# First two MLP pairs with eight plain products, residual added by accumulating transfers, residual stream kept in the output (hybrid decoder layer, 1024 tokens)

## Chip, cores and metric

One core of one Trainium2 chip runs the kernel. The metric is device time of one execution in microseconds (us); lower is better. Engines: PE is TensorE, DVE VectorE, ACT ScalarE, POOL GpSimd, SP SyncE, which here only issues transfers.

## The reference

One decoder layer over T = 1024 tokens of D = 1024 features, in float32. A mixer (S5 state space group and short convolution group) ends in an output projection, a norm and a residual add; a gated MLP with a convolution of width 3 over time follows:

```python
y = concatenate([head_rms_norm(y_a, ...), head_rms_norm(y_b, ...)], axis=-1)
x = x + gt1 * rms_norm(y @ w_out[i], g_post_mix[i])
h = rms_norm(x, g_pre_ffn[i]) * (1.0 + sc2) + sh2
hid = causal_dwconv(h @ w_up, ffn_conv_w)      # w_up: 1024 x 5632
a, v = split(hid, 2)
x = x + gt2 * rms_norm((silu(a) * v) @ w_down, g_post_ffn[i])   # w_down: 2816 x 1024
```

## The kernel before

**Arithmetic.** A float32 product is made of three fast products, high x high, high x low, low x high (`mm3`, L472; lines 476, 478, 480). So every operand is split: a cast gives the high half (weights: ACT, L462 or L1888), a subtraction the low half (DVE or POOL). A split weight tile of 128 x 1024 lies in a buffer `hl` (three of them), its raw form in a buffer `w` ("raw", three of them).

**Layout and order.** Features lie on partitions, tokens along the columns. The whole program is written by generators (`t_...`), each with a priority; a scheduler (`Flow`, L202) steps them by an internal list of costs and so writes one static order of instructions for each engine. An instruction that waits holds up all that stand behind it on its engine. Generators wait for events (`fire`) and for slots of buffers (`get`, `put`); `yield ("land",)` waits until a transfer has landed, and `SITES` (L89) says which engines a tensor operation may go to.

**Output projection and residual.** It goes by three token blocks (`blocks`): block 0 is the first token half (512 columns), blocks 1 and 2 are the quarters of the second half. `t_out` does the products of a block (weights `w_out` streamed for each block), squares and sums give the norm, and `t_x2` (L1700) makes the new residual `og` for two features groups at once (1024 or 512 columns): scale `og`, add x, square into the tile `xr` (ACT, L1710), store `og` to the scratch `x2_dr`, and sum the squares. x has been loaded before by SP into the tables `CL`, `Tr`, `Tz`, `St`, which are `xr` (`t_xr`, L1682). The sum over features is a matmul with a ones column (L492), its broadcast another (L502). `t_h2` (L1651) then gives the MLP's input, split into `h2h` and `h2l`.

**MLP, up.** 22 pairs: pair i has a tile a (128 columns of `w_up`) and a tile b (128 columns, the gated part), each with two halves of K, and the input has two token halves: a 2 x 2 block product. With Winograd's form of Strassen's scheme it takes seven products of 12 matmuls with 512 columns, not eight. The input blocks used are A11 and A12 (first token half, K halves), A22, and the sums S1 to S4 (`t_forms`); block A21 is only part of sums. The weights need sums too (`t_pair_weights`, L1901): differences on `w`, from them `wf` (split of the sum T2, for the product with S2), `hm` (split of the sum t, for S1 and A22) and the split of tile b. `t_combine` (L2011) adds the products up. For pairs 0 and 1, `t_ahead` (L1758) puts the products of A11 and A12 with tile a before the rest, since they need only the first token half; pair 0's remaining products are done in two halves of 256 columns, one for each block. `t_conv2` and `t_gate2` do the convolution (`cv`), silu and product; `t_sums` writes the results to the scratch `g_dr`.

**Residual, transposed.** The output has tokens on partitions. `t_x2t` (L2091) therefore loads pieces of `x2_dr`, transposes them on PE (16 groups of four transposes, spread over the first MLP pairs), copies each on ACT (`xt`), and stores it to the scratch `x2t_dr`.

**MLP, down.** `t_down` (L2220) does seven products in a row, P4 last, for four token groups `tb` each; w_down comes as `wd` (by SP and by POOL, L2195), split into `wh` and `wl` (DVE, L868). In the last product each token group keeps its last `LATE` = 3 steps of K for the end, so that the groups end one after the other. For each of the eight output rows of tiles `t_final` (L2329) loads the residual, waits for the halves, and does residual + u * r on DVE (L871, one for each 512 columns), and SP stores it.

Of the kernel before, what the change touches and what calls it, by code (L numbers as in the profile page):

```python
# [11 lines left out]
F32 = mybir.dt.float32  # L12
# [6 lines left out]
P = 128  # L19
# [295 lines left out]
def hybrid_layer(ctx, tc, xT, w_adaT, w_ada0, w_u, w_bcv, w_out, w_up, w_down, glu_w, vec, ssm, con, out):  # L315
# [17 lines left out]
    fl = Flow({"k2": NK2, "k4": NK4, "hl": NHL, "raw": NRAW, "big": 3, "sm": 2, "nrm": 2, "s4": 0, "sn": 0, "wf0": 0, "wf1": 0, "hm0": 0, "hm1": 0, "cv": 0, "gs": 0, "t5": 0, **{t: 1 for t in tables}})  # L333
# [97 lines left out]
    x2t_dr = tc.dram_tile([NB, P, D], F32, name="x2t_dr")  # L431
# [1088 lines left out]
    forms = {name: [[None, None] for _ in range(NT)] for name in ("A11", "A12", "A22", "S1", "S2", "S3", "S4")}  # L1520
# [128 lines left out]
    def t_h2(bi, k, og, r2b, left):  # L1649
# [33 lines left out]
    def t_xr():  # L1683

        yield ("wait", ev_stat["a"])
        for bi, (hf, lo, hi) in enumerate(blocks):
            n = hi - lo
            for dp in range(NT):
                tag = ("CL", "Tr", "Tz", "St")[dp]
                yield ("get", tag)  # L1690
                xr = table(tag, [1024])[:, : 2 * n]
                yield L_(n)
                load(
                    xr.rearrange("p (a t) -> p a t", a=2),
                    xT[2 * dp * P : (2 * dp + 2) * P, hf * H + lo : hf * H + hi].rearrange("(a p) t -> p a t", a=2),
                )
                ev_xr[bi][dp].tile = xr, tag
                fl.fire(ev_xr[bi][dp], True)

    def t_x2(bi, dp, sl, n, og, r1, s2):  # L1700
# [7 lines left out]
        yield from T_("x2", og, og, xr, ADD, 2 * n)  # L1708
# [25 lines left out]
    NAHEAD = 2  # L1734
    for i in range(NAHEAD):
        want(("up", i), w_up[i])
# [10 lines left out]
    def product(o, w, form, last, s=None):  # L1747

        for k in range(NT):
# [5 lines left out]
            mm3([o], w[0][:, ks], w[1][:, ks], [f[0]], [f[1]], k == 0, k == NT - 1)  # L1755
            if last and s != 0:
                fl.put("s4" if form == "S4" else "k2", 2)

    def t_ahead():

        yield ("wait", ev_out)
        for i in range(NAHEAD):
            w = wev["up", i]
            yield ("wait", w[0])
            hl = w[1]
            yield ("get", "big", 2 - i)
            pair_a[i] = big()
            if i == 0:
                pair_b[i] = big()
            for j, o, c, form in ((1, (pair_a if i else pair_b)[i][:, H:], 0, "A11"), (2, pair_a[i][:, :H], 1, "A12")):  # L1770
                yield from product(o, [hl[:, x, c * H : (c + 1) * H] for x in range(2)], form, False)
                ev_p[i, j].tile = o
                fl.fire(ev_p[i, j])
            fl.put("hl")
# [29 lines left out]
    NCV, NGS, NSN = 5, 2, 2  # L1804
# [60 lines left out]
    def t_forms2(s, dp, a11, a12, a21, a22):  # L1865
# [3 lines left out]
        for d2 in range(2):  # L1869
            yield from form_parts("S3", 2 * dp + d2, s, a21[:, d2], None)  # L1870
        yield from dve_tt(a12, a12, a11, SUB, H)
        for d2 in range(2):
            yield from form_parts("S4", 2 * dp + d2, s, a12[:, d2], None)
        forms_left[0] -= 1
# [6 lines left out]
    def odd_even(what, i):  # L1881

        return ptile("ba"[i % 2 == 0], what, [2, 1024 if what == "hm" else H], F32R)
# [17 lines left out]
    def t_pair_weights(i):  # L1901
        ev = pw[i]
        yield ("wait", pw[i - 1]["loaded"] if i else wev["up", NAHEAD - 1][2])
# [8 lines left out]
        if i:  # L1912
            yield ("wait", pw[i - 1]["t"])
        if i >= NAHEAD:
            yield ("get", "hl")
            ev["a"].tile = hl_tile()
            yield from split(ev["a"].tile, wa, 1024, "split_a")
            fl.fire(ev["a"])
        b11, b21, b12, b22 = wa[:, :H], wa[:, H:], wb[:, :H], wb[:, H:]

        yield from TT_("wsum" if i else "split_d", b11, b12, b11, SUB, H)
        yield from TT_("wsum" if i else "split_d", b12, b22, b12, SUB, H)
# [4 lines left out]
        yield from TT_("wsum" if i else "split_d", b22, b22, b11, SUB, H)  # L1927
        yield ("get", f"wf{i % 2}")
        ev["T2"].tile = odd_even("wf", i)
        yield from split(ev["T2"].tile, b22, H)  # L1930
        fl.fire(ev["T2"])
        yield from TT_("wsum" if i else "split_d", b21, b21, b22, SUB, H)
        fl.put("raw")
        yield ("get", f"hm{i % 2}")
        ev["t"].tile = odd_even("hm", i)
# [4 lines left out]
    def subs(i):  # L1940

        return ((0, slice(0, 256)), (1, slice(256, H))) if i == 0 else ((None, slice(0, H)),)

    snap = {(i, x): Event() for i in range(NFF) for x in ("a", "b")}

    def t_up(i):
        ev = pw[i]
        last = i == NFF - 1

# [4 lines left out]
        outs = {}  # L1954

        def one(j, o, x, c, form, s, sl):
            yield ("wait", ev[x])
            yield from product(o[:, sl], part(x, c), form, last, s)
            if s != 0:
                ev_p[i, j].tile = o  # L1960
                fl.fire(ev_p[i, j])

        def single(j, x, c, form, s, sl):
            if not s:
                yield ("get", "sm")
                outs[j] = small()
            yield from one(j, outs[j], x, c, form, s, sl)

        if i < NAHEAD:
            yield ("wait", ev_p[i, 2])  # L1970
        else:
            yield from single(1, "a", 0, "A11", None, slice(0, H))
        for s, sl in subs(i):
            yield from single(6, "T2", 0, "S2", s, sl)
            if s != 0:
                fl.put(f"wf{i % 2}")
            yield from single(5, "t", 0, "S1", s, sl)
            if i >= NAHEAD:
                yield ("get", "big")
                pair_a[i] = big()  # L1980
                yield from one(2, pair_a[i][:, :H], "a", 1, "A12", None, slice(0, H))
                fl.put("hl")
            else:
                yield ("wait", ev_s1[i])
                yield from one(4, pair_a[i][:, H:], "t", 1, "A22", s, sl)
            if i not in pair_b:
                yield ("get", "big")
                pair_b[i] = big()
            yield from one(3, pair_b[i][:, :H], "b", 1, "S4", s, sl)
            yield from one(7, pair_b[i][:, H:], "b", 0, "S3", s, sl)  # L1990
            if s != 0:
                fl.put("hl")
            if i >= NAHEAD:
                yield from one(4, pair_a[i][:, H:], "t", 1, "A22", s, sl)
            if s != 0:
                fl.put(f"hm{i % 2}")

    def t_combine(i):
# [3 lines left out]
        su = ptile("a", "sn", [2, H], F32, NSN)  # L2002
# [3 lines left out]
        fl.fire(ev_s1[i])  # L2006
        if i >= NAHEAD:
            fl.put("sm")
# [20 lines left out]
    def cv(s):  # L2029
        return ptile("b", "cv", [T], F32, NCV)  # L2030

    def t_conv2(j, o):

        yield ("get", "cv")
        r = cv("cv")
# [7 lines left out]
    ev_gs = {(f, kk): Event() for f in FORM for kk in range(NKK)}  # L2043

    def t_gate2():
        even = None
        for i in range(NFF):
            yield ("wait", snap[i, "b"])
            b = yield from t_conv2(NFF + i, pair_b[i])
# [425 lines left out]
```

## Time and profile before

| what | value |
|---|---|
| time, median of 3 runs | 1159.94 us (1154.72 to 1162.32) |
| profiled execution: its time, and the span of the trace | 1158.81 us, 1157.0 us |
| busy share PE, DVE, ACT, POOL | 91%, 77%, 41%, 41% |
| mean granted TensorE clock, as a share of full speed | 0.954 |
| mean DMA rate | 152 GB/s |

The time of the profiled execution stands 1.8 us above its span. In time lines a row gives the start, the duration, the engine, the line, and output<-input; in brackets stands the idle time before it and what ended it. Matmul durations overlap, so their rate is read from their starts. "x4" is a row for four like instructions in a row, with their total.

### The profile page before, as it was taken

The numbers are of one execution on the slowest core, as the hardware profiler recorded it, in microseconds if no ns is written. First come the engines' busy times: TensorE is split into PE (matmuls) and PEld (weight loads), VectorE is DVE, ScalarE is ACT, GpSimd is POOL, SyncE is SP. The second block draws the span as 40 slices with busy tenths as digits, with TensorE's granted clock in tenths as the row PEclk, the third lists the DMA queues.
The fourth block names the chain that finished last, engine by engine and source line by source line (L and its number), as shares of the span: only waits on it lengthen the run. The fifth ranks groups of instructions, "written<-read, shape, count | busy, mean of one in ns | idle before, by whom it ended". The sixth has DMA issues, their size and how long they took to land. (4 is left out here: it accounts for less than half of the span.)

```text
span 1157.0 us, 13979 instructions
## 1 busy us (share of the span) xinstructions
PE 1049.7 (91%) x5000; PEld 849.2 (73%) x5000; DVE 893.4 (77%) x1237; ACT 476.1 (41%) x658; POOL 471.8 (41%) x464
## 2 busy tenths in 40 slices
PE   2888889899889988659999999999999999999995
PEld 2756678778546887557788888888888887888883
DVE  6769777887997389877787888888879977554855
ACT  4435422323244446444443434343434545454431
POOL 4799455671495034113534343434344320232000
PEclk9979889999898998769999999999999999999998
DMA  7633302237645256313463333233313698999344
GB/s 266 233 131 134 119 30 88 96 114 245 246 164 182 76 187 203 127 39 106 156 200 100 119 109 110 74 119 109 110 69 123 214 247 275 239 231 275 111 160 158
DMA packets 89973, 176.26 MB, mean 152 GB/s; under 512 B 8880, under 2 KB 34224, under 8 KB 89904
## 3 DMA queue, kind: packets, MB, share of 16 engines
q1 hardware_dynamic: 83568, 163.84, 41.0%
q0 software_dynamic: 6336, 11.54, 5.8%
q8 instruction: 39, 0.64, 0.2%
q14 instruction: 30, 0.25, 0.1%
HBM read 137.89 MB, written 37.46 MB: 152 GB/s over the span
## 5 line engine op out<-in xcount | busy, mean ns | idle before, releaser
L381 POOL TENSOR_TENSOR hl<-w,hl 128x1024 fp32r<-128x1024 f32 x38 | 98.4, 2590 | 245.0 <-ACT hl L1888 143.2
L381 POOL TENSOR_TENSOR w<-w,w 128x512 f32<-128x512 f32 x63 | 93.7, 1488 | 126.4 <-DVE hl L868 81.5
L871 DVE SCALAR_TENSOR_TENSOR cv<-big,vec,cv 128x896 f32<-128x896 f32 (+3 forms) x176 | 122.7, 741 | 4.1 <-ACT cv L2037 4.1
L1888 ACT CAST hl<-w 128x1024 fp32r<-128x1024 f32 (+1 forms) x67 | 68.6, 1024 | 53.9 <-issue 17.0
L2195 POOL DMA_DIRECT2D wd<-in_w_down_dram x44 | 38.6, 897 | 112.2 <-PE big L2244 29.4
L868 DVE TENSOR_TENSOR wl<-wd,wh 128x512 fp32r<-128x512 f32 x77 | 50.9, 687 | 36.3 <-ACT wh L2199 36.3
L476 PE MATMUL big<-s,hl 128*128 128x512 f32 (+1 forms) x184 | 71.2, 387 | 0.7 <-ACT xt L2110 0.7
L868 DVE TENSOR_TENSOR hl<-w,hl 128x1024 fp32r<-128x1024 f32 (+1 forms) x47 | 55.4, 1178 | 19.9 <-ACT hl L1888 19.9
L478 PE MATMUL big<-s,hl 128*128 128x512 f32 (+1 forms) x184 | 70.7, 384 | 0.0
L480 PE MATMUL big<-s,hl 128*128 128x512 f32 (+1 forms) x184 | 70.6, 384 | 0.0
L478 PE MATMUL big<-yl,hl 128*128 128x256 f32 (+1 forms) x192 | 63.8, 332 | 4.3 <-POOL yl L381 4.3
L2199 ACT CAST wh<-wd 128x512 fp32r<-128x512 f32 x77 | 46.4, 619 | 50.9 <-DMA wd<-in_w_down_dram 49.8
L476 PE MATMUL big<-yh,hl 128*128 128x256 f32 (+1 forms) x192 | 65.6, 342 | 1.3 <-ACT hl L462 1.1
L2037 ACT ACTIVATE cv<-big,vec 128x1024 f32<-128x1024 f32 x44 | 49.2, 1119 | 42.4 <-DVE big L868 33.6
L476 PE MATMUL big<-h,hl 128*128 128x512 f32 x192 | 63.0, 410 | 3.3 <-ACT h L724 1.5
L480 PE MATMUL big<-yh,hl 128*128 128x256 f32 (+1 forms) x192 | 63.8, 332 | 2.0 <-POOL hl L381 2.0
L480 PE MATMUL big<-h,hl 128*128 128x512 f32 x192 | 61.0, 400 | 2.8 <-POOL hl L381 2.8
L478 PE MATMUL big<-h,hl 128*128 128x512 f32 x192 | 60.9, 398 | 3.0 <-DVE h L726 3.0
L462 ACT CAST hl<-w 128x1024 fp32r<-128x1024 f32 x41 | 42.8, 1045 | 43.8 <-PE big L480 28.2
L868 DVE TENSOR_TENSOR hm<-w,hm 128x1024 fp32r<-128x1024 f32 (+1 forms) x39 | 45.9, 1177 | 11.3 <-ACT hm L1888 11.3
L2242 PE MATMUL big<-wh,hl 128*128 128x512 f32 x130 | 50.9, 391 | 1.3 <-DVE sn L868 0.8
L2244 PE MATMUL big<-wh,hl 128*128 128x512 f32 x130 | 50.8, 391 | 0.5 <-DVE hl L868 0.5
(351 smaller groups left out, 3114.2 us busy)
## 6 DMA issues: line engine op xcount, KB each, us to landing
w<-in_w_up_dram SPq DMA_DIRECT2D x46, 512.0 KB, 3.9
w<-g_dr SPq DMA_DIRECT2D x35, 512.0 KB, 5.6
g_dr<-cv SPq DMA_DIRECT2D x55, 256.0 KB, 2.3
wd<-in_w_down_dram SPq DMA_DIRECT2D x44, 256.0 KB, 6.8
wd<-in_w_down_dram POOLq DMA_DIRECT2D x44, 256.0 KB, 6.7
w<-in_w_out_dram SPq DMA_DIRECT2D x20, 512.0 KB, 3.5
WBT<-in_w_adaT_dram SPq DMA_DIRECT2D x16, 512.0 KB, 4.5
w<-in_w_bcv_dram SPq DMA_DIRECT2D x13, 512.0 KB, 3.4
```

The costliest lines, as they stand in the source:

```text
L381: {"dve": dve, "pool": pool}[e].tensor_tensor(o, a, b, op)
L462: act.copy(t[:, 0, :], w)
L476: pe.matmul(outs[i], wh, xh[i], start=start, stop=False)
L478: pe.matmul(outs[i], wh, xl[i], start=False, stop=False)
L480: pe.matmul(outs[i], wl, xh[i], start=False, stop=stop)
L868: (eng or dve).tensor_tensor(o, a, b, op)
L871: dve.scalar_tensor_tensor(o, a, s, b, op0, op1)
L1888: act.copy(t[:, 0, :n], w)
L2037: act.activation(r, o, AF.Copy, scale=V("ffn_conv_w", 3 * j + 2))
L2199: act.copy(hi, w)
L2242: pe.matmul(o, gh, wh, start=kk == 0, stop=False)
L2244: pe.matmul(o, gl, wh, start=False, stop=kk == NKK - 1)
```

## The change

1. *Eight plain products in pairs 0 and 1.* No weight sums, no combining: each pair's output is the plain sum of K halves in the same accumulator (A11 with A12, A22 with A21). The form A21 is now also made as a split. `t_ahead` does A11 and A12 for (pair 0, a), (0, b), (1, a); `t_first` the rest. Weight sums start with pair 2, whose order of products is 1624537 rather than 1652374, and whose sums run on DVE (site `split_d`).
2. *Residual added by transfers in blocks 0 and 1.* `t_xr` loads no x for them; `t_x2` issues from POOL a transfer of x that adds into `og`, and waits until it has landed. Block 2 is as before.
3. *Residual kept in the output.* `t_x2t` stores the transposed residual straight into the output. `t_final` scales on ACT and a POOL transfer adds the result into the output. The transposes take a small PSUM buffer. `LATE` is 7.
4. *Buffers.* Convolution tiles: 3 `cv` and 2 `ca` instead of 5 `cv`; `sn` moves to the later pool; S4 is formed before S3.

```diff
@@ t_h2
-        if hf and k < NT:
-            fl.fire(ev_h2[bi][k])
-            return
-        name = "A22" if hf else ("A11", "A12")[k // NT]
+        name = f"A{hf + 1}{k // NT + 1}"
@@ t_xr
-                yield L_(n)
-                load(
-                    xr.rearrange("p (a t) -> p a t", a=2),
...
+                if bi == 2:
+                    yield L_(n)
+                    load(xr.rearrange("p (a t) -> p a t", a=2), x_of(bi, dp))
@@ t_x2
-        yield from T_("x2", og, og, xr, ADD, 2 * n)
+        if bi == 2:
+            yield from T_("x2", og, og, xr, ADD, 2 * n)
+        else:
+            yield ("load", "pool", 1.0)
+            pool.dma_start(o3, x_of(bi, dp), accum_op=ADD)
+            yield ("land",)
@@ t_ahead
-        for i in range(NAHEAD):
...
+        for i, x, pair in ((0, "a", pair_a), (0, "b", pair_b), (1, "a", pair_a)):
...
+            for c, form in ((0, "A11"), (1, "A12")):
+                yield from product(pair[i][:, :H], [hl[:, y, c * H : (c + 1) * H] for y in range(2)], form, False, start=c == 0, stop=c == 1)
@@ new
+    def t_first():
...
+        for s in range(2):
+            for form in ("A22", "A21"):
+                for x in "ab":
+                    yield from part(0, x, form, slice(H + s * 256, H + s * 256 + 256), s)
...
+        for form in ("A22", "A21"):
+            yield from part(1, "a", form, slice(H, T), None)
...
+        for form in ("A22", "A21", "A11", "A12"):
+            yield from part(1, "b", form, slice(H, T) if form[1] == "2" else slice(0, H), None)
@@ t_up
+        order = {2: "1624537"}.get(i, "1652374")
@@ t_x2t
-                    x2t_dr[2 * h : 2 * h + 2, :, 2 * dp * P : (2 * dp + 2) * P].rearrange("b p d -> p b d"),
+                    outB[2 * h : 2 * h + 2, :, 2 * dp * P : (2 * dp + 2) * P].rearrange("b p d -> p b d"),
@@
-    LATE = 3
+    LATE = 7
@@ t_final
-        x = cv("x")
-        yield L_(512)
-        load(x, x2t_dr[b])
...
-            stt(x[:, sl], u, r, x[:, sl], MUL, ADD)
...
-            load(outB[b, :, sl], x[:, sl])
+            yield A_(H + 100)
+            act.activation(u, u, AF.Copy, scale=r)
+            yield ("load", "pool", 1.0)
+            pool.dma_start(outB[b, :, c * H : (c + 1) * H], u, accum_op=ADD)
```

ScalarE in block 0 of the output projection, before: the squares (L1710, into `CL`, `Tr`, `Tz`, `St`) alternate with the casts of the next block's weights (L462) and with the evacuation of its products (L1605, L1607).

```order
L1710 ACTIVATE CL_2777<-og_2941 128x1024
L462 CAST hl_3254<-w_3157 128x1024
L1710 ACTIVATE Tr_2790<-og_2975 128x1024
L1605 ACTIVATE og_3279<-big_3213,col 128x256 x2
L1607 ACTIVATE oq_3280<-big_3213 128x512
L462 CAST hl_3292<-w_3197 128x1024
L1710 ACTIVATE Tz_2802<-og_3010 128x1024
L1605 ACTIVATE og_3350<-big_3281,col 128x256
L1710 ACTIVATE St_2814<-og_3070 128x1024
```

Now:

```order
L1713 ACTIVATE CL_2776<-og_2936 128x1024
L1713 ACTIVATE Tr_2777<-og_2970 128x1024
L1604 ACTIVATE og_3275<-big_3208,col 128x256
L1713 ACTIVATE Tz_2778<-og_3005 128x1024
L1604 ACTIVATE og_3275<-big_3208,col 128x256
L461 CAST hl_3266<-w_3152 128x1024
L1606 ACTIVATE oq_3276<-big_3208 128x512
L1713 ACTIVATE St_2779<-og_3065 128x1024
L461 CAST hl_3314<-w_3192 128x1024
```

Two weight casts have moved behind the third and the fourth square (`Tz`, `St`); in the changed kernel a line's number is one less from L432 on, and three more at the squares.

TensorE at the opening of the MLP, before: behind the products of the first token half (`h2h`, `h2l` with `hl`) stand the norm sums of block 2, and then half-wide products of a sum `s` with `wf`.

```order
L476 MATMUL big_3865<-h2h_3706,hl_3751 128x512
L478 MATMUL big_3865<-h2l_3707,hl_3751 128x512
L480 MATMUL big_3865<-h2h_3706,hl_3751 128x512
L492 MATMUL sm_3933<-con,CL_3686 128x1 x4
L502 MATMUL sm_3954<-con,nrm_3940 128x128 x2
L476 MATMUL sm_3866<-s_3786,wf_3967 128x256
L478 MATMUL sm_3866<-s_3787,wf_3967 128x256
L480 MATMUL sm_3866<-s_3786,wf_3967 128x256
L476 MATMUL sm_3866<-s_3806,wf_3967 128x256
```

Now, at the end of the six products of the first token half:

```order
L475 MATMUL big_3903<-h2h_3600,hl_3800 128x512
L477 MATMUL big_3903<-h2l_3601,hl_3800 128x512
L479 MATMUL big_3903<-h2h_3600,hl_3800 128x512
L475 MATMUL big_3774<-h2h_3689,hl_3694 128x256
L477 MATMUL big_3774<-h2l_3690,hl_3694 128x256
L479 MATMUL big_3774<-h2h_3689,hl_3694 128x256
L475 MATMUL big_3774<-h2h_3705,hl_3694 128x256
```

What follows the first token half is a half-wide product of A22 with the weights themselves; no product with `wf` stands there.

VectorE at the first `wf` in its order, which is pair 0's before:

```order
L868 TENSOR_TENSOR s_663_4013<-og_3070,s_662_4012 128x256
L871 SCALAR_TENSOR_TENSOR s_3879<-og_3129,tsh,s_3878 128x256
L868 TENSOR_TENSOR s_3870<-og_3350,s_3869 128x256
L868 TENSOR_TENSOR wf_3967<-w_3753,wf_3967 128x512
L868 TENSOR_TENSOR s_3923<-og_3350,s_3922 128x256
L868 TENSOR_TENSOR s_3931<-og_3279,s_3930 128x256
L868 TENSOR_TENSOR og_3010<-og_3010,og_2941 128x2x256
```

Now it is pair 2's:

```order
L867 TENSOR_TENSOR w_3844<-w_3844 128x512
L867 TENSOR_TENSOR s_4311<-og_3275,s_4310 128x256 x2
L867 TENSOR_TENSOR hl_4317<-w_3844,hl_4317 128x1024
L867 TENSOR_TENSOR w_3844<-w_3844,w_3843 128x512
L870 SCALAR_TENSOR_TENSOR cv_4336<-big_4197,vec,cv_4336 128x896
L867 TENSOR_TENSOR wf_4345<-w_3844,wf_4345 128x512
L870 SCALAR_TENSOR_TENSOR cv_4336<-big_4197,vec,cv_4336 128x127
```

`wf` has moved behind the split `hl` of pair 2's tile b and between the taps of a convolution (`cv` from `big`, pair 1's tile b).

## Rows read from the trace of the kernel before

**Rows 1.** By stage: busy us (count) of PE, PEld, DVE, ACT, POOL; clock; DMA share; GB/s

```profile
480.00:500.00 20.00, 5.18 (x24) 3.64 (x22) 19.12 (x44) 10.05 (x24) 0.00 (x0) 0.68 0.23 79
...
500.00:520.00 20.00, 15.36 (x103) 14.77 (x104) 12.80 (x25) 7.70 (x16) 5.14 (x4) 0.73 0.15 54
...
700.00:800.00 100.00, 100.00 (x437) 81.87 (x436) 86.78 (x101) 39.18 (x44) 41.40 (x26) 1.00 0.31 108
```

**Rows 2.** TensorE's waits: us in total, times, longest

```profile
PE sm L480 <- DVE wf L868: 13.2, 1, 13.2
...
PE sm L492 <- DVE CL L381: 2.7, 1, 2.7
```

**Rows 3.** TensorE in order of time, projection's end and MLP opening

```profile
429.31 1.84 PE L492 MATMUL sm<-con,CL 128*128 128x1 f32 x8 [4.78 <-issue]
...
463.89 0.39 PE L476 MATMUL big<-h2h,hl 128*128 128x512 f32 x1
...
503.40 0.58 PE L480 MATMUL sm<-s,wf 128*128 128x256 f32 x1 [13.23 <-DVE wf L868]
...
511.29 0.28 PE L476 MATMUL big<-h2h,hm 128*128 128x256 f32 x1
```

**Rows 4.** TensorE in order of time, first matmuls of pairs 2, 3 and 4

```profile
537.01 0.39 PE L476 MATMUL sm<-h2h,hl 128*128 128x512 f32 x1
...
559.27 0.39 PE L476 MATMUL sm<-h2h,hl 128*128 128x512 f32 x1
...
580.43 0.39 PE L476 MATMUL sm<-h2h,hl 128*128 128x512 f32 x1
```

**Rows 5.** VectorE in order of time, projection and MLP opening

```profile
413.17 3.42 DVE L381 TENSOR_TENSOR og<-og,Tr 128x1024 f32<-128x1024 f32 x1
...
418.77 1.21 DVE L381 TENSOR_TENSOR og<-og,Tz 128x1024 f32<-128x1024 f32 x1
...
492.56 1.67 DVE L871 SCALAR_TENSOR_TENSOR h2l<-og,mod,h2h 128x256 fp32r<-128x256 f32 x4
...
494.14 3.69 DVE L868 TENSOR_TENSOR og<-og,og 128x512 f32<-128x512 f32 x6
...
512.82 1.23 DVE L868 TENSOR_TENSOR hl<-w,hl 128x1024 fp32r<-128x1024 f32 x1 [3.92 <-ACT hl L1888]
...
526.58 1.14 DVE L871 SCALAR_TENSOR_TENSOR cv<-big,vec,cv 128x896 f32<-128x896 f32 x1
...
548.37 2.71 DVE L871 SCALAR_TENSOR_TENSOR cv<-big,vec,cv 128x896 f32<-128x896 f32 x4
```

**Rows 6.** ScalarE's cast of a weight tile; POOL's splits, two in a row

```profile
511.73 1.05 ACT L1888 CAST hl<-w 128x1024 fp32r<-128x1024 f32 x1 [4.17 <-POOL w L381]
...
409.51 6.00 POOL L381 TENSOR_TENSOR hl<-w,hl 128x1024 fp32r<-128x1024 f32 x2 [36.36 <-ACT hl L462]
```

**Rows 7.** `wd` issues by POOL, their landings, `wl` beside them, transfers to landing

```profile
L2195 POOL DMA_DIRECT2D wd<-in_w_down_dram x44: 856/872/1215, 917.6 to 1058.4; - x44
...
DMA to landing us min/median/max: 3.9/6.7/9.4
...
L868 DVE TENSOR_TENSOR wl<-wd,wh x77: 680/685/694, 916.6 to 1087.5; 128x512 fp32r<-128x512 f32 x77
...
Tz<-in_xT_dram SPq DMA_DIRECT2D x1, 512.0 KB, 13.9
...
out_dram<-cv SPq DMA_DIRECT2D x16, 256.0 KB, 2.0
```

**Rows 8.** All engines in order of time, the end

```profile
1137.14 0.69 DVE L868 TENSOR_TENSOR sn<-big,sn 128x512 f32<-128x512 f32 x1 [9.63 <-PE big L2244]
...
1137.93 0.63 ACT L2266 ACTIVATE gs<-sn 128x512 f32<-128x512 f32 x1 [16.13 <-DVE sn L868]
...
1143.29 0.40 PE L2244 MATMUL sm<-wh,hm 128*128 128x512 f32 x1
...
1153.31 0.74 DVE L871 SCALAR_TENSOR_TENSOR cv<-s,fin,cv 128x512 f32<-128x512 f32 x1
```

More of the change, by code (lines that the diff above doesn't have):

```diff
@@ L1745, in hybrid_layer, with product @@
     ev_s1 = [Event() for _ in range(NFF)]
-    def product(o, w, form, last, s=None):
+    def product(o, w, form, last, s=None, start=True, stop=True):
         for k in range(NT):
@@ L1754, in product @@
             yield M_(0.687 if s is None else 0.345)
-            mm3([o], w[0][:, ks], w[1][:, ks], [f[0]], [f[1]], k == 0, k == NT - 1)
-            if last and s != 0:
+            mm3([o], w[0][:, ks], w[1][:, ks], [f[0]], [f[1]], start and k == 0, stop and k == NT - 1)
+            if last:
                 fl.put("s4" if form == "S4" else "k2", 2)
+    first_hl = {}
+    ev_ahead = {x: Event() for x in ((0, "a"), (0, "b"), (1, "a"))}
     def t_ahead():
         yield ("wait", ev_out)
-        for i in range(NAHEAD):
-            w = wev["up", i]
+        for i, x, pair in ((0, "a", pair_a), (0, "b", pair_b), (1, "a", pair_a)):
+            w = wev["up", i + NFF * (x == "b")]
             yield ("wait", w[0])
[L1765 to L1774, printed above, removed]
+            first_hl[i, x] = hl = w[1]
+            yield ("get", "big")
+            pair[i] = big()
+            for c, form in ((0, "A11"), (1, "A12")):
+                yield from product(pair[i][:, :H], [hl[:, y, c * H : (c + 1) * H] for y in range(2)], form, False, start=c == 0, stop=c == 1)
+            fl.fire(ev_ahead[i, x])
     fl.spawn(t_small(), PRIO["t_small"])
@@ L1873, in t_forms2 @@
             yield from form_parts("S4", 2 * dp + d2, s, a12[:, d2], None)
+        for d2 in range(2):
+            yield from form_parts("S3", 2 * dp + d2, s, a21[:, d2], None)
         forms_left[0] -= 1
@@ L1952, in part, with one @@
             return t[:, 0, c * H : (c + 1) * H], t[:, 1, c * H : (c + 1) * H]
-        outs = {}
-        def one(j, o, x, c, form, s, sl):
+        def one(j, o, x, c, form):
             yield ("wait", ev[x])
[L1958 to L1979, printed above, removed]
-                pair_a[i] = big()
-                yield from one(2, pair_a[i][:, :H], "a", 1, "A12", None, slice(0, H))
-                fl.put("hl")
[L1983 to L1996, printed above, removed]
+            yield from product(o, part(x, c), form, last)
@@ new lines, in one, with single, pa @@
+            ev_p[i, j].tile = o
+            fl.fire(ev_p[i, j])
+        def single(j, x, c, form):
+            yield ("get", "sm")
+            yield from one(j, small(), x, c, form)
+        def pa():
+            if i not in pair_a:
+                pair_a[i] = big()
+            return pair_a[i]
+        order = {2: "1624537"}.get(i, "1652374")
+        for j in map(int, order):
+            if j in (1, 5, 6):
+                yield from single(j, *{1: ("a", 0, "A11"), 5: ("t", 0, "S1"), 6: ("T2", 0, "S2")}[j])
+            elif j in (2, 4):
+                if i not in pair_a:
+                    yield ("get", "big")
+                yield from one(j, pa()[:, H * (j == 4) :][:, :H], *{2: ("a", 1, "A12"), 4: ("t", 1, "A22")}[j])
+            else:
+                if j == 3:
+                    yield ("get", "big")
+                    pair_b[i] = big()
+                yield from one(j, pair_b[i][:, H * (j == 7) :][:, :H], "b", int(j == 3), ("S3", "S4")[j == 3])
+            if j == 6:
+                fl.put(f"wf{q}")
+            elif j in (2, 7):
+                fl.put("hl")
@@ L2373, in t_all_up @@
     def t_all_up():
-        for i in range(NFF):
+        yield from t_first()
+        for i in range(2, NFF):
             yield from t_up(i)
@@ L2381, in hybrid_layer @@
             fl.spawn(t_forms(s, dp), PRIO["forms"][s])
-    for i in range(NFF):
+    for i in range(2, NFF):
         fl.spawn(t_pair_weights(i), PRIO["weights"])
@@ L2386, in hybrid_layer @@
     fl.spawn(t_gate2(), PRIO["t_gate2"])
-    for i in range(NFF):
+    for i in range(2, NFF):
         fl.spawn(t_combine(i), PRIO["t_combine"])
```

151 lines of the change are left out of this document (82 added, 69 removed).

## The prediction

> **What bounds the kernel now.** I read the views in this order: busy time by stage, TensorE's waits, TensorE in order of time, then VectorE and the transfers in the stages where TensorE waits.
>
> In the middle of the program TensorE is the bound: between 700 and 800 us it is busy all the time, 437 matmuls in 100 us, 0.229 us for one of 512 columns [rows 1]. A regular MLP pair has 84 of them, 19.2 us. There only fewer matmuls would help. Two other places have gaps. From 480 to 500 us TensorE works 5.18 of 20 us while VectorE works 19.12 [rows 1]; the longest wait of the MLP's opening is 13.2 us for VectorE's `wf`, the first weight sum of pair 0 [rows 2], and another 4.8 us lie in the output projection, ahead of 429.31 [rows 3]. The reader is to see three things in the order of time: the MLP starts at 463.89, its second half only goes on at 503.40, and pair 2 starts at 537.01 and ends at 559.27 [rows 3, 4]. At the end the last matmul runs to 1143.7, and VectorE still finishes at 1154 and the span at 1157.0: a tail of 13.3 us [rows 8].
>
> What the 13.2 us hide: the last token block's normalised input `h2l` is written from 492.56 to 494.2 [rows 5]. Until then no MLP product of the second token half can start, whatever its form. Only the rest, 494.2 to 503.4, is the price of the sums.
>
> **The change, part by part.** The sum is made against the profiled execution, 1158.81 us (span 1157.0); the median of the runs is 1159.94, 1.1 us above it.
>
> *Opening of the MLP.* Removed: for pairs 0 and 1 the weight sums, their splits and the combining adds. Added: one product of 12 matmuls in each pair, 24 x 0.229 = 5.5 us of TensorE. Moved: six products (72 matmuls, 16.5 us) instead of four now need the first token half alone and stand ahead; four half-wide groups (48 of 256 columns, 0.115 us each as half of 0.229, 5.5 us) need block 1 only. That is 22 us of work that is ready before the last block, where there were 11.
>
> The last block's chain (squares, two norms, residual, scaling) keeps its links, so I leave it at 30.3 us after the projection's end, 463.9 to 494.2. TensorE in that window: 22 us of products, some 8 us of waits in order (2.7 of them for `CL` [rows 2], the others alike), 2 us of small norm products: 32 us, so it arrives at 496 and block 2 is ready. What is left of the two pairs is 192 - 72 - 24 = 96 matmuls, 22.0 us, and three transpose groups of the residual. Such a group costs 0.64 us: pair 3 with three of them took 580.43 - 559.27 = 21.16 us [rows 4] against 19.24 for 84 matmuls. So pair 2 starts at 496 + 22.0 + 1.9 = 519.9 instead of 537.0.
>
> Then a wait that is new. Pair 2's second product needs its own `wf`. In VectorE's new order `wf` stands behind a convolution tap of pair 1's second tile, which needs that tile's last matmul, and behind the split `hl`, whose ScalarE cast stands behind a residual copy that waits for a transpose nine matmuls into pair 2. From 519.9: nine matmuls 2.1, transposes 0.6, the copy 0.6 (a ScalarE instruction over 512 columns takes 0.63 [rows 8]), cast 1.05, split 1.23, difference 0.69, tap 1.14, `wf` 0.69 (this and the difference as the subtraction of 512 columns in rows 8) [rows 5, 6, 8]: 528.0. TensorE has finished the first product at 519.9 + 2.75 = 522.7, so it waits 5.3 us. VectorE's own list by then is 50 instructions after the last `h2l`: eleven of 512 columns at 0.615, 24 of 256 at 0.42, three conv tiles at 2.71 and a tap at 1.14, two of 1024 at 1.2 [rows 5]: 28.5 us, to 522.7, so it is not what ends last, but with only 5 us to spare.
>
> [...] I take 3 us after the 5.3 us wait. Pair 2 ends at 528.0 + 72 x 0.229 + 3 + three more transpose groups 1.9 = 549.4, against 559.27: 9.9 us gained. Four of the sixteen transpose groups fewer are left for the pairs behind it, 4 x 0.64 = 2.5 us.
>
> Pairs 3 to 21 and the down projection are the same instructions; VectorE has 13% free there [rows 1], and the two conv pools hold five tiles as the one did. Cost nothing, if pair 3's weights come in time.
>
> *Residual by transfers in blocks 0 and 1.* Removed: eight adds on VectorE, 1.21 us for 1024 columns when POOL is quiet and up to 3.42 beside POOL work [rows 5, 6]. Added: eight accumulating transfers, 512 KB in block 0 and 256 KB in block 1, with a POOL issue of 0.87 us each. The one that the trace shows, 256 KB of w_down, lands 3.9 to 9.4 us after its issue, median 6.7 in a stage with heavy traffic; the longest plain load of 512 KB of x took 13.9 us [rows 7]. I take 5 to 6 us, nearest to the low end, as the traffic of this stage is between. The new wait stands on ScalarE: the squares of block 0 wait for the landing, and the casts of the next output weights stand behind them. By this, the weight split that TensorE needs at 416 us, POOL's of 409.51 [rows 6], comes some 5 us late; but TensorE stood 4.8 us anyway until 429.31 for the same block's sum [rows 3], which is then ready. For block 1 the eight instructions that the form A21 adds (4 casts, 4 `h2l` of 0.42) stand against the four adds removed. I take 0 for this stage, between -5 (all stretching gone) and +8 (landing at 9.4).
>
> [...]
>
> *The output.* Removed: the loads of the residual, and sixteen multiply-adds on VectorE, the last at 1153.31 [rows 8]. Added: sixteen ScalarE scalings and sixteen accumulating stores of 256 KB from POOL. Eight of them belong to the first four token groups and end under the last product. With seven late steps instead of three, groups 4 to 6 end 14.4, 9.6 and 4.8 us ahead of the last matmul, so only one group is left behind it: subtraction 0.7, square 0.8 with its accumulator, product with the column vector 0.7, five small norm steps 1.2, two scalings 1.2, second issue at +5.0, landing 3.9 to 4.2 later, and 0.9 to the span's end as today: 10.1 instead of 13.3 us, 3.2 gained. Bounds: landing as a plain output store, 2.0, gives 5.1; 9.4 gives a loss of 2.3 [rows 7].
>
> Sum: 9.9 + 2.5 + 0 + 3.2 = 15.6 us, 1158.8 - 15.6 = 1143.
>
> **The rivals.** 1. *More is gained*: the wait for pair 2's `wf` does not come, as TensorE arrives later than I think or the copies earlier: 5.3 + 3 less, 1135. For it: my chain hangs on one transpose. Against: the order stands as written. 2. *The wait is passed on*: pair 3 is fed late too, as VectorE and the three raw weight buffers are as late as pair 2's, one more wait of 5.3 and 3 us: 1151. For it: VectorE worked 19.12 of 20 us just before [rows 1] and has 5 us to spare. Against: it frees 13% of each later pair. 3. *The transfers take over, and it is slower than before*: each block's squares are released by its last landing. At 13.9 us [rows 7] instead of 5.5 that is 8.4 later in both blocks, 17 us, and nothing else fills TensorE as its casts stand behind the squares: 1160, and 1165 with 9.4 us in the tail. It decides from 16 us later in the projection's end. Against: the queue has no 2 MB burst of loads there any more. 4. *The issues hold VectorE up*, 3.42 - 1.21 = 2.2 us for each of the eight: 1161. The `wl` row speaks against it.
>
> **How the numbers follow.** Forecast 0.52, rival 1 0.20, rival 2 0.16, rival 3 0.09, rival 4 0.03. The forecast's own range is 1137 to 1149 (stage of the projection and landing in the tail); with rival 1 down to 1131 and rivals 2 and half of 3 and 4 up to 1157 about 0.2 is left out. One per cent (11.6 us), about what a measurement of this kernel can tell from no change, lies at 1148.3 and 1171.5: faster holds rival 1 and nearly all of the forecast less its upper edge, 0.66; same the edge, rival 2 and most of 3 and 4, 0.29; slower 0.05.
>
> **What would show it.** Right: no wait of over 10 us in TensorE's list; pair 2 starting 16 to 18 us after where h2 of the last block is read instead of 34; one wait of about 5 us for `wf` early in pair 2 with a granted clock under 0.9 there; accumulating loads of x landing in 4 to 7 us; the projection ending near 464; the tail near 10 us with the last issue on POOL. Wrong: the projection ending past 475 with ScalarE waiting for transfers, VectorE instructions of 3 us beside POOL issues, or waits over 3 us in pairs 3 to 5.

## The result and the profile after

The changed kernel takes 1167.52 us (median of 8 runs, 1161.29 to 1169.37) against 1159.68 us before (8 runs, 1154.72 to 1162.32): ratio 1.0063, 95% interval 1.0043 to 1.0082. It is slower, by a little; 1143 was forecast. The profiled execution took 1169.3 us with a span of 1167.5, 10.5 us over the span of before.

TensorE in order of time, after: the waits in the output projection, the first matmul of the MLP, the first matmuls of pairs 2, 3 and 4 with the wait inside pair 2, and the last matmul.

```profile
430.86 0.58 PE L475 MATMUL big<-yh,hl 128*128 128x256 f32 x1 [13.11 <-ACT hl L461]
...
470.06 0.58 PE L479 MATMUL big<-yh,hl 128*128 128x256 f32 x1 [11.60 <-POOL hl L381]
...
488.13 0.39 PE L475 MATMUL big<-h2h,hl 128*128 128x512 f32 x1
...
541.91 0.39 PE L475 MATMUL sm<-h2h,hl 128*128 128x512 f32 x1
...
552.35 0.79 PE L475 MATMUL sm<-s,wf 128*128 128x512 f32 x1 [6.72 <-ACT wf L1889]
...
572.56 0.40 PE L475 MATMUL sm<-h2h,hl 128*128 128x512 f32 x1
...
593.29 0.39 PE L475 MATMUL sm<-h2h,hl 128*128 128x512 f32 x1
...
1155.34 0.40 PE L2266 MATMUL sm<-wh,hm 128*128 128x512 f32 x1
```

Against [rows 3, 4, 8] this is the whole account, milestone by milestone:

| stretch | before | after | gained (+) or lost (-) |
|---|---|---|---|
| to the MLP's first matmul | 463.89 | 488.13 | -24.2 |
| from there to pair 2 | 73.1 | 53.8 | +19.3 |
| pair 2 | 22.3 | 30.65 | -8.4 |
| pair 3 to the last matmul's end | 584.4 | 583.2 | +1.2 |
| tail to the span's end | 13.3 | 11.8 | +1.5 |

The sum is -10.5. The opening and the tail gained as the plan wanted; the projection lost more than both. The wait of 13.2 us for `wf` [rows 2] is gone from the opening, and two waits of 13.1 and 11.6 us stand in the projection, where the longest before was 4.8 [rows 3]. Where they come from stands on POOL and ScalarE. POOL in order of time, the four issues of block 0 (512 KB each):

```profile
409.96 1.40 POOL L1710 DMA_DIRECT2D og<-in_xT_dram  x1 [35.72 <-ACT og L1604]
415.93 1.24 POOL L1710 DMA_DIRECT2D og<-in_xT_dram  x1 [4.57 <-issue]
422.17 1.21 POOL L1710 DMA_DIRECT2D og<-in_xT_dram  x1 [5.00 <-issue]
428.75 1.22 POOL L1710 DMA_DIRECT2D og<-in_xT_dram  x1 [5.38 <-issue]
```

ScalarE at the same time, the squares that wait for the landings, and the weight cast that stands behind the third:

```profile
415.69 1.06 ACT L1713 ACTIVATE CL<-og 128x1024 f32<-128x1024 f32 x1 [4.26 <-DMA og<-in_xT_dram]
...
421.93 1.06 ACT L1713 ACTIVATE Tr<-og 128x1024 f32<-128x1024 f32 x1 [5.18 <-DMA og<-in_xT_dram]
...
428.45 1.06 ACT L1713 ACTIVATE Tz<-og 128x1024 f32<-128x1024 f32 x1 [5.10 <-DMA og<-in_xT_dram]
...
429.77 1.03 ACT L461 CAST hl<-w 128x1024 fp32r<-128x1024 f32 x1
...
436.81 1.06 ACT L1713 ACTIVATE St<-og 128x1024 f32<-128x1024 f32 x1 [5.51 <-DMA og<-in_xT_dram]
```

The landings of all eight loads, from the view of that line:

```profile
DMA to landing us min/median/max: 4.2/5.3/8.0
```

The two lists are to be read together. Each load of block 0 lands 5.7 to 8.1 us after its issue (the square that it releases starts then), not far from the forecast. But POOL issues the next one only 0.24 to 0.30 us after the one before has landed, though VectorE had scaled all four `og` by 413.4. "Issue" as the reason means that POOL waited for nothing that the profile shows. So block 0's residual takes four landings in a row, 409.96 to 436.81, and the weight cast behind `Tz` comes at 429.77; TensorE's wait ends with it at 430.86. Block 1 repeats it with 256 KB each (452.15 to 470.66). There the weight split that TensorE needs stands on POOL itself, behind the fourth issue, and the second wait ends with it at 470.06:

```profile
466.41 1.22 POOL L1710 DMA_DIRECT2D og<-in_xT_dram  x1 [3.31 <-issue]
467.17 2.83 POOL L381 TENSOR_TENSOR hl<-w,hl 128x1024 fp32r<-128x1024 f32 x1
```

TensorE's clock beside the stall is in the stage view of 420 to 440 us (columns as in [rows 1]): 36 matmuls, and a granted clock of 0.57 of full speed, where the same 20 us of before have 104 and 0.83.

```profile
420.00:440.00 20.00, 7.34 (x36) 6.84 (x36) 5.77 (x5) 7.46 (x11) 4.16 (x3) 0.57 0.78 185
```

### The profile page after: what moved, and what is told of

It reads as the page before. It is cut to its first block, busy times and chain, and to the rows that moved or that the text cites. A ratio compares the mean times of both kernels' runs of the same rounds, so it can differ in the third digit from the quotient of the medians.

```text
span 1167.5 us, 13965 instructions
## 1 busy us (share of the span) xinstructions
PE 1056.0 (90%) x5012; PEld 855.6 (73%) x5012; DVE 877.8 (75%) x1212; ACT 486.7 (42%) x676; POOL 473.6 (41%) x475
## 4 chain that ended last, share of the span: by engine, by line
PE 44%; POOL 15%; issue 15%; DVE 12%; DMA 9%; ACT 3%; SPq 1%; POOLq 0%; DVEq 0%; ACTq 0%
PE big L475 9%; PE big L477 9%; PE big L479 9%; PE sm L475 5%; PE sm L479 5%; PE sm L477 5%; DMA wd<-in_w_down_dram 3%; POOL pa L381 2%; DMA w<-g_dr 2%; POOL Pt L381 1%; POOL wd L2217 1%; POOL out_dram L2366 1%; POOL pt L894 1%; POOL yl L381 1%; POOL pt L900 1%
## 5 line engine op out<-in xcount | busy, mean ns | idle before, releaser
L381 POOL TENSOR_TENSOR hl<-w,hl 128x1024 fp32r<-128x1024 f32 x34 | 86.8, 2554 | 253.6 <-ACT hl L1889 145.6
L381 POOL TENSOR_TENSOR w<-w,w 128x512 f32<-128x512 f32 x57 | 86.3, 1514 | 83.1 <-DVE hl L867 80.1
L475 PE MATMUL big<-yh,hl 128*128 128x256 f32 (+1 forms) x192 | 67.7, 352 | 13.3 <-ACT hl L461 13.1
L479 PE MATMUL big<-yh,hl 128*128 128x256 f32 (+1 forms) x192 | 65.9, 343 | 13.0 <-POOL hl L381 11.6
L870 DVE SCALAR_TENSOR_TENSOR ca<-big,vec,ca 128x896 f32<-128x896 f32 (+1 forms) x92 | 65.1, 740 | 4.5 <-ACT ca L2055 4.5
L867 DVE TENSOR_TENSOR hl<-w,hl 128x1024 fp32r<-128x1024 f32 (+1 forms) x45 | 52.8, 1174 | 14.6 <-ACT hl L1889 14.6
L475 PE MATMUL big<-s,hl 128*128 128x512 f32 x160 | 63.2, 395 | 0.0
L477 PE MATMUL big<-s,hl 128*128 128x512 f32 x160 | 63.1, 394 | 0.0
L479 PE MATMUL big<-s,hl 128*128 128x512 f32 x160 | 62.9, 393 | 0.0
L870 DVE SCALAR_TENSOR_TENSOR cv<-big,vec,cv 128x896 f32<-128x896 f32 (+1 forms) x84 | 58.3, 739 | 5.3 <-ACT cv L2055 5.3
L475 PE MATMUL big<-h2h,hl 128*128 128x512 f32 (+1 forms) x160 | 60.4, 378 | 0.0
L479 PE MATMUL big<-h2h,hl 128*128 128x512 f32 (+1 forms) x160 | 59.6, 373 | 0.7 <-DVE hl L381 0.7
L477 PE MATMUL big<-h2l,hl 128*128 128x512 f32 (+1 forms) x160 | 59.6, 373 | 0.0
```

Source lines behind the costliest of these rows:

```text
L381: {"dve": dve, "pool": pool}[e].tensor_tensor(o, a, b, op)
L475: pe.matmul(outs[i], wh, xh[i], start=start, stop=False)
L477: pe.matmul(outs[i], wh, xl[i], start=False, stop=False)
L479: pe.matmul(outs[i], wl, xh[i], start=False, stop=stop)
L867: (eng or dve).tensor_tensor(o, a, b, op)
L870: dve.scalar_tensor_tensor(o, a, s, b, op0, op1)
```

## The experiments

The theory after the result: POOL's queue for its transfers has little room, an accumulating load of 256 rows fills it, and the next issue waits until there is room, that is for a landing. In `kernel()` stands `dynamic_dma_scratch_size=1024`, which the theory takes for the bytes of that room, a line that the change does not touch. Rivals: accumulating loads into SBUF go one at a time by nature, or another part of the change holds the projection up.

**e1: x added on an engine again.**

```diff
-        if bi == 2:
-            yield from T_("x2", og, og, xr, ADD, 2 * n)
-        else:
-            yield ("load", "pool", 1.0)
-            pool.dma_start(o3, x_of(bi, dp), accum_op=ADD)
-            yield ("land",)
+        yield from T_("x2", og, og, xr, ADD, 2 * n)
```

(`t_xr` loads x for every block again.)

> The changed kernel with part 2 undone: x of blocks 0 and 1 is loaded by SP into the tables again and added on an engine, as block 2 is. Theory (the transfers alone hold the projection up): the 24.2 us by which the first MLP matmul came later (488.1 against 463.9) come back, the projection ends at 462 to 468, and the time is 1143 to 1150 us; the wait for pair 2's wf stays at 5 to 8 us. Rival (the later projection comes from another part, such as the order of the forms, the pools or weight loads put off): the projection still ends past 480 and the time stays at 1160 to 1168.

Measured: 1145.96 us, ratio to before 0.9872 (0.9848 to 0.9896). TensorE in order of time: the first matmul of the MLP, `wf` in pair 2, pair 3, the last matmul.

```profile
461.67 0.59 PE L475 MATMUL big<-h2h,hl 128*128 128x512 f32 x1
...
527.19 0.79 PE L475 MATMUL sm<-s,wf 128*128 128x512 f32 x1 [4.11 <-ACT wf L1883]
...
547.72 0.39 PE L475 MATMUL sm<-h2h,hl 128*128 128x512 f32 x1
...
1131.46 0.40 PE L2260 MATMUL sm<-wh,hm 128*128 128x512 f32 x1
```

The projection ends at 461.7 instead of 488.1, and the wait for `wf` is 4.1 us, a little under what I wrote. So the loss lies in the eight transfers alone, and the rest of the change gains 15.6 us.

**e2 and e3: the same program with little and with more room.** To leave bytes for the larger room, both take one constant tile (`exps`, 2 KB) from the `k2` buffers; they differ in one number.

```diff
-    nc = _bacc.Bacc("TRN2", ..., dynamic_dma_scratch_size=1024)
+    nc = _bacc.Bacc("TRN2", ..., dynamic_dma_scratch_size=3072)
```

> The changed kernel with one constant tile of 2 KB per partition (exps) taken from the k2 buffers, so that room is left; nothing else, and the scratch for GpSimd's transfers is 1024 bytes as before. It is the control for the next run. Both theories: 1163 to 1171 us, accumulating loads one behind the other as in the changed kernel, some 6 us apart in block 0.

> The control with the scratch for GpSimd's transfers set to 3072 bytes instead of 1024; the same instructions. Theory (GpSimd's next issue waits until there is room for its rows, which is when the transfer before has landed): the four issues of block 0 go out within 1.5 us of each other, block 0's last square comes 10 to 16 us earlier, TensorE's waits of 13.1 and 11.6 us shrink by 15 to 24 us in all, and the time is 1145 to 1155 us. Rival (accumulating loads into SBUF are done one at a time whatever the room, or another wait in the program orders them): issues 6 us apart as in the control, and the time the same within 3 us.

Measured: 1170.17 us (ratio to before 1.0073, 1.0049 to 1.0097) and 1147.56 us (0.9896, 0.9858 to 0.9935). POOL's issues in block 0 with 1024 bytes:

```profile
409.47 1.40 POOL L1715 DMA_DIRECT2D og<-in_xT_dram  x1 [35.68 <-ACT og L1609]
415.68 1.24 POOL L1715 DMA_DIRECT2D og<-in_xT_dram  x1 [4.82 <-issue]
...
428.83 1.22 POOL L1715 DMA_DIRECT2D og<-in_xT_dram  x1 [5.50 <-issue]
```

and with 3072, all four of block 0 in one row and all four of block 1 in the next, then ScalarE's last square of block 0 and TensorE's first matmul of the MLP:

```profile
407.78 5.17 POOL L1715 DMA_DIRECT2D og<-in_xT_dram  x4 [35.65 <-ACT og L1609]
436.86 4.90 POOL L1715 DMA_DIRECT2D og<-in_xT_dram  x4
...
423.79 1.06 ACT L1718 ACTIVATE St<-og 128x1024 f32<-128x1024 f32 x1 [1.15 <-DMA og<-in_xT_dram]
...
466.00 0.40 PE L475 MATMUL big<-h2h,hl 128*128 128x512 f32 x1
```

No wait stands between the issues, the last square of block 0 comes at 423.79 instead of 437.00, and 22.6 us are back (the four issues take 5.2 us, not 1.5 as I had written). This settles the cause: not the landing of a load, and not accumulation by nature, but the room behind which POOL holds its next issue. With that room the time can't be told from that with the adds (1147.6 against 1146.0), but in the profiled runs the projection still ends 4.3 us later (466.0 against 461.7). Four accumulating loads under way at once also land later, 8.8 us (median of the 512 KB ones) against 6.1 one at a time. And one VectorE instruction with both operands in SBUF (`h2l`, from 438.49) took 6.22 us instead of 0.74 there, beside issues and a split on POOL; which of the two slowed it is not shown.

**e4: the same loads in halves of 128 rows.**

```diff
-            pool.dma_start(o3, x_of(bi, dp), accum_op=ADD)
+            xs = x_of(bi, dp)
+            for a_ in range(2):
+                pool.dma_start(o3[:, a_, :], xs[:, a_, :], accum_op=ADD)
```

> The changed kernel with each accumulating load of x issued as two, one for each 128 rows, so 16 instead of 8. Theory (room for rows): the second half of a pair goes out at once behind the first, with no wait for a landing, and three or four halves are under way at a time as in the stores of the tail; block 0 takes 12 to 20 us instead of 27, the time is 1150 to 1164 us. Rival (one at a time): the halves come 4 to 5 us apart, block 0 takes over 32 us, and the time is over 1175 us.

Measured: 1157.4 us, ratio 0.9965 (0.9948 to 0.9983). POOL's issues, first three rows of block 0 and first two of block 1:

```profile
407.16 2.87 POOL L1712 DMA_DIRECT2D og<-in_xT_dram  x3 [35.76 <-ACT og L1604]
411.85 0.88 POOL L1712 DMA_DIRECT2D og<-in_xT_dram  x1 [1.81 <-DVE hl L381]
414.14 0.87 POOL L1712 DMA_DIRECT2D og<-in_xT_dram  x1 [1.41 <-issue]
...
439.42 2.67 POOL L1712 DMA_DIRECT2D og<-in_xT_dram  x3
444.55 2.68 POOL L1712 DMA_DIRECT2D og<-in_xT_dram  x3 [2.47 <-issue]
```

Three halves go out back to back, then POOL waits 2.47 us, then three more. The same bytes in smaller pieces use the room better, and some 10 us come back. It is not the bytes that fill the room: in the changed kernel one load of 512 KB went at a time in block 0, and one of 256 KB in block 1; here three of 128 KB did in block 1, 384 KB together.

**e9: the same loads without accumulation** (told here, out of the order of the runs).

```diff
-            pool.dma_start(o3, x_of(bi, dp), accum_op=ADD)
+            pool.dma_start(o3, x_of(bi, dp))
```

> The changed kernel with the eight transfers of x as plain loads over og instead of accumulating ones: the addition is left out (the residual is x alone), the order and every wait are the same. It tells what takes the room. Theory A (an accumulating transfer takes room for each of its rows twice, to read the old contents too): two or three plain loads of 256 rows go out back to back, block 0 is done in 10 to 16 us instead of 27, the time is 1148 to 1158 us. Theory B (rows alone count): still one at a time, 4.5 to 6 us apart, and the time within 4 us of the changed kernel's 1167.

Measured: 1142.14 us, ratio 0.9827 (0.9792 to 0.9861; two executions), which is below the range that I wrote. Block 0 and block 1 on POOL:

```profile
406.95 1.81 POOL L1710 DMA_DIRECT2D og<-in_xT_dram  x2 [35.77 <-ACT og L1604]
409.11 0.72 POOL L1710 DMA_DIRECT2D og<-in_xT_dram  x1 [0.36 <-issue]
411.38 0.73 POOL L1710 DMA_DIRECT2D og<-in_xT_dram  x1 [1.54 <-issue]
...
432.52 2.16 POOL L1710 DMA_DIRECT2D og<-in_xT_dram  x3
```

Theory B (rows alone count) is refuted: three plain loads of 256 rows are under way at once where one accumulating load was, and the last square of block 0 comes 11.2 us after the first issue. Theory A's count fits: counted by rows, an accumulating one takes more than one and a half times the room of a plain one (three plain loads fit, two accumulating ones do not). That this is for reading the old contents is not shown. Its issue costs 1.21 us against some 0.73 in the issues that stand alone.

How 1024 bytes come to just these counts is not shown: no trace shows how many bytes a row takes.

**e5 and e10: the old end of the output.** For all eight rows of tiles the residual is loaded by SP, multiplied and added on VectorE and stored by SP; e5 keeps `LATE = 7` and three buffers, e10 has `LATE = 3` and five.

```diff
+            load(x, outB[b])
+            yield ("land",)
...
-            act.activation(u, u, AF.Copy, scale=r)
...
-            pool.dma_start(outB[b, :, c * H : (c + 1) * H], u, accum_op=ADD)
+            stt(x[:, sl], u, r, x[:, sl], MUL, ADD)
+            load(outB[b, :, sl], x[:, sl])
```

> The kernel of the run with the residual added on an engine (e1), and the end of part 3 undone too: for all eight rows of tiles the residual is loaded from the output by SP, multiplied and added on VectorE, stored by SP, as before the change; seven late steps stay. Theory (part 3 gains what the tail shows, 13.3 us before against 11.6 in e1): 1.5 to 3 us slower than e1, 1147.5 to 1149. Rival (the tail is shorter by the seven late steps alone, and the slow landing of GpSimd's accumulating stores, 3.9 to 5.2 us against 2.0, gives the rest back): as fast as e1 or up to 2 us faster, 1144 to 1146.

> e1 with the old end entire: residual loaded by SP, multiplied and added on VectorE, stored by SP, LATE = 3, and five conv tiles (three cv, two ca) to load into, as before the change. So only part 1 is left, with the buffers and the residual kept in the output. In e5 three tiles and seven late steps put the loads behind the stores, a tail of 22.4 us. Theory (part 3 is worth the difference of the tails, 13.3 against 11.6): tail 12.5 to 14.5, time 1146.5 to 1149.5. Rival (the old end needs what the new kernel no longer has, the early loads): tail over 17, time over 1150.

Measured: 1154.62 us (0.9958, 0.9938 to 0.9979) and 1154.94 us (0.9928, 0.9905 to 0.9951), tails of 22.4 and 18.8 us. Both miss the theory; for e10 the rival came, a tail over 17 us for want of early loads. In e5 too the chain that ended last goes through a late load of the residual. In all engines in order of time of e10, that load goes out 8.5 us behind the last matmul's end, and VectorE waits for it.

```profile
1142.59 0.34 SPq L360 DMA_DIRECT2D cv<-out_dram  x1
...
1148.30 1.42 DVE L870 SCALAR_TENSOR_TENSOR cv<-s,fin,cv 128x512 f32<-128x512 f32 x2 [2.82 <-DMA cv<-out_dram]
```

My order of the buffers made that load wait for a store to land (issued at 1138.61, 3.9 us); before, the last such load was at 1145.00, 1.3 us behind the last matmul's end. So these runs are no clean undoing of part 3, and what part 3 alone is worth against the old end stays open; the tails of before and after (13.3 and 11.8) are all that bears on it.

**e6: the last row of tiles alone by SP.** The edit of e5 for row 7 only; the other seven accumulate.

> e1 with the last row of tiles alone done in the way before (load of the residual ahead, multiply and add on VectorE, two stores by SP); the other seven accumulate into the output. Theory (what stands last is the landing of two accumulating stores, issued one behind the other by GpSimd): the tail falls from 11.6 to 7.5 to 9.5 us, the time to 1142 to 1144.5. Rival (the landing is hidden or the load of x comes late): 1145 to 1148.

Measured: 1139.51 us, ratio 0.982 (0.9791 to 0.9849), against 0.9872 for e1. The end, all engines in order of time: last matmul, last accumulating issue, last two stores; the span is 1129.5 (the profiled execution was the fastest of the six, 1131.28, so only stretches of it are compared).

```profile
1121.22 0.40 PE L2260 MATMUL sm<-wh,hm 128*128 128x512 f32 x1
...
1121.85 1.17 POOL L2380 DMA_DIRECT2D out_dram<-wf  x1
...
1125.68 1.00 SPq L360 DMA_DIRECT2D out_dram<-cv  x2
```

The tail falls from 11.6 to 7.9 us, as the theory said: what stood last was the landing of GpSimd's stores. The last issue stands 4.7 us behind the last matmul's end instead of 5.0, and its store lands in 2.3 us instead of 5.4. The time is below the range that I wrote: the medians differ by 6.4, and the other 2.7 lie within what executions of one kernel differ by here (1131.28 to 1140.71 for e6).

**e7: `LATE = 3`.**

```diff
-    LATE = 7
+    LATE = 3
```

> e1 with LATE = 3 instead of 7. Theory (the groups of the last product end 2 us apart instead of 4.8, so more than one row's finish is behind the last matmul): the tail is 13 to 16 us, the time 1147.5 to 1151. Rival (only the last row matters, whatever the others do): within 1 us of e1.

Measured: 1151.93 us, ratio 0.9938 (0.9916 to 0.996), a tail of 18.6 us (last matmul's start 1135.11, span 1154.1), both above what I wrote. The mark of the full room shows here a second time, on POOL behind the last matmul:

```profile
1143.02 0.88 POOL L2360 DMA_DIRECT2D out_dram<-sn  x1 [1.66 <-issue]
1144.30 0.88 POOL L2360 DMA_DIRECT2D out_dram<-wf  x1 [0.40 <-issue]
1145.58 0.86 POOL L2360 DMA_DIRECT2D out_dram<-sn  x1 [0.41 <-issue]
1147.82 0.86 POOL L2360 DMA_DIRECT2D out_dram<-wf  x1 [1.37 <-issue]
```

ScalarE had scaled the last tile by 1141.4; the stores queue up behind each other. The room was not varied here, so this stays a reading of the rows. Seven late steps keep the groups 4.8 us apart (in e1 the last two pairs of issues start at 1131.49 and 1136.27, both when ScalarE has scaled `sn`), and so, by this reading, within the room: the part of the change that I counted as a detail is worth 7 us of tail once the stores accumulate.

**e8 and e11: another order of pair 2's products**, in e1 and in e6.

```diff
-        order = {2: "1624537"}.get(i, "1652374")
+        order = {2: "1237654"}.get(i, "1652374")
```

> e1 with pair 2's products in the order 1, 2, 3, 7, 6, 5, 4 instead of 1, 6, 2, 4, 5, 3, 7: four products that need no weight sum stand ahead of the one that needs wf. Theory (the wait for wf in pair 2, 4.1 us in e1, and the low clock behind it are a loss of the new order): the wait for wf goes, pair 3 starts 5 to 8 us earlier than e1's 547.7, the time is 1139 to 1142. Rival (VectorE is as late with what pair 3 needs, or a buffer is not free, so that the wait moves on): pair 3 or 4 waits 3 us or more, the time is within 2 us of e1.

> The kernel of the last row by SP (e6, 1139.5) with pair 2's products in the order 1, 2, 3, 7, 6, 5, 4 (e8). Theory (e8 moved the wait from pair 2 to pair 3 and to the transposes and gave 0 to 2 us): 1137 to 1140, as e6 within 2 us, tail 7 to 9. Rival (the order is worth its 4 us wait): 1134 to 1136.5.

Measured: 1143.7 us (0.987, 0.9845 to 0.9895; e1 0.9872) and 1140.05 us (0.9807, 0.9777 to 0.9837; e6 0.982). In e8 pair 3 starts at 541.26, 6.5 us before e1's 547.72, as the theory said, but the wait moved on to pair 3's `wf`. TensorE, that wait and the first matmul of pair 4:

```profile
548.62 0.80 PE L475 MATMUL sm<-s,wf 128*128 128x512 f32 x1 [2.05 <-ACT wf L1883]
...
569.60 0.39 PE L475 MATMUL sm<-h2h,hl 128*128 128x512 f32 x1
```

With it come two waits for loads of the residual in pair 3 (1.77 and 1.65 us) and slow matmuls (0.80 us for the first with `wf`, 0.39 for the first of pair 4). From the start of pair 2 to that of pair 4 it is 50.87 us (from 518.73), and 50.88 in e1 (517.40 to 568.28): nothing is saved, and the rival holds. e6 and e11 are the fastest versions, about 28 us below the changed kernel, and 19 to 23 below before as it ran beside them.

## Why the prediction was wrong

*The step that failed* is the term "residual by transfers in blocks 0 and 1": I took 0 for the stage, between -5 and +8, and it lost 24.2 us. I had the landing nearly right (5 to 6 us forecast, medians of 6.1 for the 512 KB loads and 4.2 for the 256 KB ones) and the consequence too, that the squares wait and the casts stand behind them. What I did not ask is how many of the four can be under way at once: the sum counted one landing for a block, there were four in a row. The trace of before shows it. Its 44 `wd` loads by POOL [rows 7] are accumulating loads of 128 rows (L2195 has `accum_op=ADD`). The same view that gave their landings has POOL's idle time ahead of them, and the issues in order of time carry the mark:

```profile
  issue: 25.0, 18
...
1011.07 0.89 POOL L2195 DMA_DIRECT2D wd<-in_w_down_dram  x1 [2.49 <-issue]
1012.46 0.87 POOL L2195 DMA_DIRECT2D wd<-in_w_down_dram  x1 [0.50 <-issue]
```

18 of the 44 issues waited with "issue" as the reason, 25.0 us in all. With each load's time to landing beside its start, never more than three are under way, and behind three the next goes out mostly some 0.3 us after the oldest has landed. Where three accumulating loads of 128 rows fit and a fourth does not, one of 256 rows fits and a second does not, if the room goes by rows: four landings in a row for a block, from rows that were there. I read how long one takes to land and not how many were under way. The 1024 bytes stand in the kernel's text besides, and the sum made no use of them.

*Rival 3* named the right place, side and mechanism in part (squares released late, casts behind them, slower), at 0.09. Its price was wrong in kind: 8.4 us more in each block by a landing of 13.9 us. The landing was short, the queue long. Its point of decision, 16 us later at the projection's end, was passed with 24.

*Right*: the opening. Forecast 56.0 us from the projection's end to pair 2, measured 53.8; the new wait for `wf` forecast at 5.3, measured 6.7, with a low clock behind it (0.50 granted from 552.3 to 556.0, 0.79 us for its first matmul); pair 2 in 29.5, measured 30.65. No run shows the 3 us that the sum took after the wait; in the changed kernel the twelve matmuls with `wf` and one transpose group took 5.4 us (552.35 to 557.76), 2.0 more than the forecast's 12 x 0.229 + 0.64. Both together 9.9 gained by forecast and 10.9 by measurement. That the wait's size came out is partly luck, as its chain was another. On ScalarE, a silu of the gate and the cast of `wf`:

```profile
546.58 1.06 ACT L2074 ACTIVATE ca<-ca 128x1024 f32<-128x1024 f32 x1 [2.95 <-DVE ca L870]
...
551.68 0.62 ACT L1889 CAST wf<-w 128x512 fp32r<-128x512 f32 x1 [0.51 <-DVE w L867]
```

The copy and the cast of `hl` stood behind that silu, which waited for VectorE's convolution; so VectorE's own list, which I had 5 us clear, was what held the chain up. And the wait ended with ScalarE's cast of `wf`, without the tap and the split on VectorE (1.14 and 0.69 us) that the sum had last. e1 has the stage without its transfers: 1143 forecast for the whole change, 1145.96 measured, pair 3 at 549.4 forecast and 547.7 measured. Its 15.6 us under before equal the forecast's sum, but in the profiled runs 13.5 us divide otherwise: 2.2 from the projection (forecast 0), 9.3 from the opening with pair 2 (9.9), 0.3 behind it (2.5) and 1.7 from the tail (3.2). With room the stage comes near its term: in e3 the projection ends 2.1 us behind before, within -5 to +8.

*Mis-sized*: the pairs behind pair 2 gave 1.2 us instead of 2.5. The tail gave 1.5 instead of 3.2; the last issue came where the sum had it, 5.0 us behind the last matmul's end (1160.76), but the store took 5.2 us to land, not 4.2, and 1.5 us instead of 0.9 lie from there to the span's end, for which no view gives a reason. (The bounds of that term were reckoned from a landing of 3.9 us, its sum from 4.2; the slip of 0.3 decides nothing.) After, the queue of those stores, with its median in us:

```profile
out_dram<-wf POOLq DMA_DIRECT2D x4, 256.0 KB, 5.2
```

*Rival 1* did not come: the wait for `wf` is there. *Rival 2* neither, in the changed kernel: pairs 3 and 4 took 20.7 and 20.3 us (pair 3 21.2 before [rows 4]). *Rival 4* did not come either: VectorE's three scalings of 1024 columns beside the first issue took 3.47 us, 1.16 each, not 3.4 each. They read `sm` from PSUM, where the add of 3.42 [rows 5] read two operands from SBUF; but in e4 instructions with both operands in SBUF (`h2l`) took 0.75 us each, both beside accumulating issues (439.42 to 442.09) and after them. The scalings, and then four `h2l` of e4 in a row:

```profile
408.08 3.47 DVE L867 TENSOR_TENSOR og<-og,sm 128x1024 f32<-128x1024 f32 x3
...
440.39 2.74 DVE L870 SCALAR_TENSOR_TENSOR h2l<-og,mod,h2h 128x512 fp32r<-128x512 f32 x4
```

## What to carry to other kernels

Before work is moved to a queue, ask not only how long one transfer takes to land but how many can be under way: the room of the queue is a resource like a buffer, and in this case an issue that waited for "issue" until right behind a landing (0.24 to 0.30 us) was the mark of a full one. The mark stood in the trace of before. Here 2 KB more of room freed the queue, and pieces of half the rows gave back some 10 us; the fastest versions (e6, e11) leave these adds to an engine. And what is issued last should use the path that lands soonest, even where the rest uses another: one row of tiles on SP instead of POOL was worth 3.7 us.

## What the runs showed of the hardware

Unexpected was how hard the room binds: with 1024 bytes one accumulating load of 256 rows at a time, three of 128 rows, three plain ones of 256 rows; with 3072 bytes four accumulating ones of 256 at least. POOL's next issue came 0.24 to 0.30 us after the landing that made the room. The addition has a price too: with up to three under way the median to landing was 6.0 us for 256 KB of x accumulating (e4) and 5.6 for 512 KB plain (e9). The wait for room was the greater price, 22.6 us from e2 to e3.
